# Router logits from the un-normalised rows, with the layer norm's root and mean entering per token behind the router

## The chip, the core and the metric

The kernel runs on one core of a Trainium2 chip. The metric is the time of one execution on the device in microseconds (us), taken as the median of several runs; lower is better. The core has five engines with instruction streams of their own: TensorE (PE) for matmuls and transposes, VectorE (DVE) and ScalarE (ACT) for elementwise work, GpSimd (POOL) as another elementwise engine, and SyncE (SP), which here issues the DMA transfers that bring the weights.

## The reference, cut to what matters

```python
def grouped_moe(x, router_w, router_bias, w_gate, w_up, w_down):
    x2 = x.reshape(-1, d)
    aff = jax.nn.sigmoid((x2 @ router_w).astype(jnp.float32))
    sel = (aff + router_bias.astype(jnp.float32)).reshape(-1, N_GROUPS, EXPERTS_PER_GROUP)
    grp_score = jnp.sum(lax.top_k(sel, 2)[0], -1)
    ...
    def step(acc, ew):
        g_e, wg_e, wu_e, wd_e = ew
        h = jax.nn.silu(x2 @ wg_e) * (x2 @ wu_e)
        return acc + (h @ wd_e) * g_e[:, None].astype(x2.dtype), None
...
    for l in range(DEPTH):
        ...
        x = layer_norm(ALPHA * x + mix, ln_mix_g[l], ln_mix_b[l])
        ffn = grouped_moe(x, router_w, router_bias, moe_w_gate[l], moe_w_up[l], moe_w_down[l])
        x = layer_norm(ALPHA * x + ffn, ln_ffn_g[l], ln_ffn_b[l])
    return x
```

There are 256 tokens of width 1024 and two layers. `mix` is a conformer convolution in layer 0 and a differential attention in layer 1. After each, a layer norm with gain and bias feeds a mixture of experts: a router of 16 columns picks two experts of one group for each token, and every expert is three matrices. A second block (a state space mixer with attention, then a feed-forward layer) follows; the change does not touch it.

## The kernel before, in words

The tokens lie as two blocks of 128 rows (`tb` 0 and 1), each row of 1024 columns handled as two halves of 512 (`nh` 0 and 1). All weights come from memory in units of 1 MB. SP issues them in the order of a fixed plan into ring buffers, as far ahead as the rings have room; a ring slot becomes free when the unit in it was used.

**Phase A** (layer 0's mixer): eight `pw1` units, for each of which ACT makes a rounded high part `wh` and POOL or DVE the remainder `wl` (L376), then PE multiplies (L381 to L383). Some columns of the depthwise convolution run on PE (`cv`, L623) with band matrices `band` that POOL writes (L599); their shifted inputs `xq` come back from memory by DMA. Then a layer norm, the projection `pw2`, and at its end the residual sum `res`.

**The head of each MoE** is what the change is about. The last unit of the last projection (`pw2` in layer 0, `wo` in layer 1) is computed as four groups of six matmuls, one for each block and half; behind each, DVE adds the group into the sum (L689 or L1218) and takes statistics (L429, L430). Behind the last group come 16 or 18 matmuls on zeros (`warm`, L359), which only keep PE at work, the variance's root (ACT's Ln and Exp L416 and L417, DVE L418 to L420), and the scaling of the rows in four halves, two on DVE (L440), two on ACT (L441). PE transposes the normalised rows (`fm_x1T`, L452), DVE (L742) and ACT (L744) put gain and bias on the way out of PSUM, and the router's matmuls (`lg`, L749) follow. Their sum is copied (`lgs`), added across four partition groups (`aff`, L754) and goes through a sigmoid. Beside it, rows are split for the experts: ACT writes the rounded `nh` (L735), DVE the remainder `nl` (L759).

**Routing** is a chain of small DVE instructions, from `sel` (L945) over ranks (`rkd_e`, `rk_e`, `rkd_g`, `rk_g`, L935 to L950) to the mask `maskb` (L956); PE makes positions of it (`pos`, L959), DVE a selection matrix `S` (L773), and PE's `px` (L787, L790) gathers the rows for the experts from `nh` and `nl`. The matrix units `u_moe` are used from the first `pg` (L812) on. No engine has other work to put under this chain.

Instructions stand on each engine in an order that is fixed when the program is built; each waits at its turn for what it needs.

Of the kernel before, what the change touches and what calls it, by code (L numbers as in the profile page):

```python
# [9 lines left out]
F32 = mybir.dt.float32  # L10
# [17 lines left out]
NE = 16  # L28
# [5 lines left out]
LN_EPS = 1e-5  # L34
# [37 lines left out]
COL_AT = {}  # L72
# [63 lines left out]
def pack(I):  # L136
    g = {k: np.asarray(v) for k, v in I.items()}
    a = {}
# [87 lines left out]
    a["wdown"] = units_q(g["w_down_2"][0])  # L226
    return {k: np.ascontiguousarray(v) for k, v in a.items()}


class Net:  # L230
# [229 lines left out]
    def build(self, phases="ABCDE"):  # L460
        tc, nc = self.tc, self.nc
        self.order(phases)
        with ExitStack() as ctx:
# [21 lines left out]
            c3 = ExitStack()  # L485
            xs = self.phase_a(late, early, c3) if "A" in phases else self.skip("n1", c3)
            for i in range(TB):
                self.dump(f"n1{i}", xs[i])
            rows = lambda l: self.rows.get(l) or self.mix_rows(l)
            if "B" in phases:  # L490
                xs, src = self.moe(0, xs, "mix_g0", "mix_b0", ["ring4", "ring5", "ring3"], rows(0))
            else:
                xs, src = self.inject("y1")
# [4 lines left out]
            self.retire = {}  # L498
            xs = self.attention(xs, c3) if "C" in phases else self.skip("n3", c3)
            for i in range(TB):  # L500
                self.dump(f"n3{i}", xs[i])
            if "D" in phases:
                xs, src = self.moe(1, xs, "mix_g1", "mix_b1", ["ring4", "ring5", "ring3", "ring2"], rows(1))
            else:
                xs, src = self.inject("y3")
# [62 lines left out]
    def phase_a(self, late, early, c3):  # L568
# [64 lines left out]
        taps, tap = conv_taps(), None  # L633
        rel_bias = self.rel_bias(e1)
        res = [self.act.tile([P, D], F32, tag=f"xacc{tb}", name=f"res{tb}") for tb in range(TB)]
        n = [self.act.tile([P, D], F32, tag=f"x{tb}", name=f"n{tb}") for tb in range(TB)]
        for j in range(KT):
# [51 lines left out]
        self.proj_q("pw2", range(4), sh, sl, lo=nc.gpsimd, done= lambda tb, nh, pp: nc.vector.tensor_tensor(  # L689
            res[tb][:, nh * 512:(nh + 1) * 512], pp, res[tb][:, nh * 512:(nh + 1) * 512], ALU.add))  # L690
        self.rows[0] = self.mix_rows(0)
        self.warm(W["l0"])
        self.norm_rows(res, "l0", AF.Sigmoid)
        late.close()
        self.open_ring(c3, "ring4", RING4)
        return res

# [24 lines left out]

    def moe(self, l, n, gname, bname, last_rings, rows):
        nc = self.nc
        with ExitStack() as ctx:
# [6 lines left out]
            for tb in range(TB):  # L732
                xnh.append(self.act.tile([P, D], FR, tag=f"x{tb}", name=f"nh_{l}{tb}"))
                xnl.append(b1.tile([P, D], FR, tag=f"nl{tb}", name=f"nl_{l}{tb}"))
                nc.scalar.activation(xnh[tb], n[tb], AF.Copy)  # L735
            g_row, b_row = rows
            x1T = b1.tile([P, KT, T], F32, tag="xe", name=f"x1T{l}")

            def evac(j, pt):
                d = x1T[:, j]  # L740
                if j // 2 % 2 == 0:
                    nc.vector.tensor_scalar(d, pt, self.col(gname, j), self.col(bname, j), op0=ALU.mult, op1=ALU.add)  # L742
                else:
                    nc.scalar.activation(d, pt, AF.Identity, bias=self.col(bname, j), scale=self.col(gname, j))  # L744
            self.to_fm(n, evac, f"x1T{l}")
            lg = self.bank(f"lg{l}")
            for k in range(KT):
                r = slice(32 * (k % 4), 32 * (k % 4) + 32)
                nc.tensor.matmul(lg[r, :T], self.col("router_w", NE * k, 32), x1T[:, k], start=k < 4, stop=k >= 4)  # L749
            lgs = b1.tile([P, T], F32, tag="h", name=f"lgs{l}")  # L750
            nc.scalar.activation(lgs, lg[:, :T], AF.Copy)
            pa = self.bank(f"aff{l}")
            for tb in range(TB):
                nc.tensor.matmul(pa[:, tb * NE:(tb + 1) * NE], lgs[:, tb * P:(tb + 1) * P], self.col("groups", 0, NE), start=True, stop=True)  # L754
            aff = b1.tile([P, TB, NE], F32, name=f"affs{l}")
            nc.scalar.activation(aff, pa[:, :TB * NE].rearrange("p (t e) -> p t e", t=TB), AF.Sigmoid)
            self.warm(W["lg"])
            for tb in range(TB):
# [3 lines left out]
            nc.gpsimd.tensor_copy(idg[:, :, :P], self.ident.unsqueeze(1).to_broadcast([P, TB, P]))  # L762
            posm, nmax, gates = self.route(l, b1, aff)
# [266 lines left out]
    def attention(self, n, c3):  # L1030
# [165 lines left out]
        for tb in range(TB):  # L1196
# [659 lines left out]
```

## Time and profile before

| | |
|---|---|
| median of 3 runs | 1167.34 us (1165.78 to 1167.7) |
| the profiled execution | 1166.63 us |
| its span, first to last instruction | 1164.9 us |
| granted TensorE clock, mean | 0.990 of full speed |
| PE busy | 1112.4 us, 95% |
| DVE, ACT, POOL busy | 631.8, 455.3, 308.1 us (54%, 39%, 26%) |
| DMA | 315.11 MB, 271 GB/s over the span |

The span is what the trace's rows sum to; 1.7 us of the execution lie outside it. PE's 95% is an average over stages with different limits: beside the weights' DMA, the span has stretches in which PE and DMA wait together for a chain of small steps.

### The profile page before, as it was taken

Reading aid. Unit: us, or ns where it says so; the run is one execution under the profiler, and the core shown is the slowest. Engines: PE = TensorE matmul, PEld = TensorE weight load, DVE = VectorE, ACT = ScalarE, POOL = GpSimd, SP = SyncE. Lnnn points to the kernel's source line nnn. Section 1 sums busy time; section 2 is a strip of 40 time slices with the busy share of each in tenths; the row PEclk is TensorE's granted clock in tenths of the full one; section 3 lists DMA queues with packets and bytes.
Section 4 is the critical chain, followed back from the end, with each engine's and each line's share of the span. In section 5 each row is a group of like instructions: output and inputs, shape, how many; then the busy total and the mean of one; then the engine's idle time right before and its main releaser. Section 6 shows DMA issues by size and latency. Waiting matters only on the chain.

```text
span 1164.9 us, 18257 instructions
## 1 busy us (share of the span) xinstructions
PE 1112.4 (95%) x7235; PEld 790.8 (68%) x7235; DVE 631.8 (54%) x1259; ACT 455.3 (39%) x798; POOL 308.1 (26%) x187
## 2 busy tenths in 40 slices
PE   9879989999999998989999999999999999999996
PEld 7857434444337997434344337989999988999996
DVE  6936721232227766721233227866988858665555
ACT  4314311011216665311011116555677566444443
POOL 5922000000003432000000005552324574444443
PEclk9989999999999999999999999999999999999998
DMA  9989489999999645599999993443323452554551
GB/s 358 308 260 403 152 364 418 420 419 421 419 415 415 238 161 218 240 372 387 419 419 421 419 418 106 161 155 118 128 92 109 173 208 73 217 181 167 196 199 55
DMA packets 53215, 315.11 MB, mean 271 GB/s; under 512 B 7111, under 2 KB 13312, under 8 KB 17024
## 3 DMA queue, kind: packets, MB, share of 16 engines
q1 hardware_dynamic: 49016, 309.02, 68.3%
q10 hardware_dynamic: 4104, 4.82, 1.3%
q8 instruction: 60, 0.98, 0.3%
q14 instruction: 35, 0.29, 0.1%
HBM read 312.01 MB, written 3.39 MB: 271 GB/s over the span
## 4 chain that ended last, share of the span: by engine, by line
PE 41%; DVE 9%; ACT 3%; DMA 1%; issue 1%; POOL 0%; ACTq 0%; DVEq 0%; POOLq 0%; SPq 0%
PE up L382 4%; PE up L383 4%; PE py L812 4%; PE up L381 4%; PE pu L812 4%; PE pg L812 3%; DVE E L1548 2%; PE pdn L383 2%; PE pdn L382 2%; PE pdn L381 2%; PE dwin L381 1%; PE dwin L382 1%; PE dwin L383 1%; DVE dwin L1342 1%; PE dwout L383 1%; PE dwout L382 1%
## 5 line engine op out<-in xcount | busy, mean ns | idle before, releaser
L812 PE MATMUL pu<-u_moe,xe 128*64 128x512 f32 x256 | 114.6, 600 | 4.7 <-PEq L991 4.7
L812 PE MATMUL py<-u_moe,hT 128*64 128x512 f32 x256 | 114.0, 596 | 1.4 <-DMA u_moe<-in_moe 0.8
L813 PE MATMUL pu<-u_moe,xe 128*64 128x512 f32 x256 | 114.7, 600 | 0.0
L813 PE MATMUL py<-u_moe,hT 128*64 128x512 f32 x256 | 113.6, 596 | 0.0
L812 PE MATMUL pg<-u_moe,xe 128*64 128x512 f32 x256 | 113.4, 593 | 0.0
L813 PE MATMUL pg<-u_moe,xe 128*64 128x512 f32 x256 | 113.0, 593 | 0.0
L881 DVE TENSOR_TENSOR h<-h,pu 128x512 f32<-128x512 f32 x16 | 11.0, 688 | 184.3 <-PE pu L813 171.6
L381 PE MATMUL dwin<-xih,wh 128*128 128x272 f32 (+1 forms) x352 | 104.8, 298 | 1.1 <-DVE xih L1288 1.1
L382 PE MATMUL dwin<-xil,wh 128*128 128x272 f32 (+1 forms) x352 | 102.1, 290 | 1.1 <-DVE xil L1289 1.1
L382 PE MATMUL up<-fxl,wh 128*128 128x258 f32 (+1 forms) x352 | 100.5, 285 | 1.6 <-DVE fxl L1729 1.6
L383 PE MATMUL dwin<-xih,wl 128*128 128x272 f32 (+1 forms) x352 | 101.5, 288 | 0.0
L381 PE MATMUL up<-fxh,wh 128*128 128x258 f32 (+1 forms) x352 | 100.4, 285 | 0.8 <-ACT fxh L1728 0.8
L383 PE MATMUL up<-fxh,wl 128*128 128x258 f32 (+1 forms) x352 | 100.4, 285 | 0.0
L376 POOL TENSOR_TENSOR wl<-u_win,wh 128x1024 fp32r<-128x1024 f32 x25 | 60.3, 2412 | 62.6 <-ACT wh L367 59.9
L916 DVE SCALAR_TENSOR_TENSOR yl<-py,gc,yh 128x512 fp32r<-128x512 f32 x32 | 24.0, 751 | 94.7 <-ACT yh L915 93.7
L812 PEld LDWEIGHTS pu<-u_moe,xe 128*64 128x64 f32 x256 | 35.1, 138 | 59.2 <-issue 58.0
L812 PEld LDWEIGHTS py<-u_moe,hT 128*64 128x64 f32 x256 | 33.4, 137 | 59.9 <-issue 56.0
L812 PEld LDWEIGHTS pg<-u_moe,xe 128*64 128x64 f32 x256 | 34.6, 137 | 54.7 <-issue 53.6
L376 POOL TENSOR_TENSOR wl<-u_wup,wh 128x1024 fp32r<-128x1024 f32 x22 | 52.8, 2401 | 64.7 <-ACT wh L367 64.7
L382 PEld LDWEIGHTS up<-fxl,wh 128*128 128x128 f32 x352 | 67.7, 192 | 2.5 <-DVE fxl L1729 1.8
L381 PEld LDWEIGHTS up<-fxh,wh 128*128 128x128 f32 x352 | 67.6, 192 | 2.0 <-ACT fxh L1728 1.3
L382 PEld LDWEIGHTS dwin<-xil,wh 128*128 128x128 f32 x352 | 67.0, 190 | 2.0 <-DVE xil L1289 1.9
(526 smaller groups left out, 3025.6 us busy)
## 6 DMA issues: line engine op xcount, KB each, us to landing
u_moe<-in_moe SPq DMA_DIRECT2D x192, 1024.0 KB, 18.6
u_win<-in_win SPq DMA_DIRECT2D x22, 1024.0 KB, 4.9
u_wup<-in_wup SPq DMA_DIRECT2D x22, 1024.0 KB, 5.3
u_pw<-in_pw SPq DMA_DIRECT2D x11, 1024.0 KB, 11.6
u_wdown<-in_wdown SPq DMA_DIRECT2D x11, 1024.0 KB, 4.9
u_wout<-in_wout SPq DMA_DIRECT2D x8, 1024.0 KB, 4.9
u_wk<-in_wk SPq DMA_DIRECT2D x4, 1024.0 KB, 15.8
u_wq<-in_wq SPq DMA_DIRECT2D x4, 1024.0 KB, 16.2
```

The lines of the kernel that those rows point to most:

```text
L376: eng.tensor_tensor(l, w, h.bitcast(F32), ALU.subtract)
L381: mm(ps, lh, rh, start=first, stop=False)
L382: mm(ps, lh, rl, start=False, stop=False)
L383: mm(ps, ll, rh, start=False, stop=last)
L812: nc.tensor.matmul(ps[0:64], a, ra, start=first, stop=last)
L813: self.upped = nc.tensor.matmul(ps[64:128], b, rb, start=first, stop=last)
L881: nc.vector.tensor_tensor(h, h, pu, ALU.mult)
L916: nc.vector.scalar_tensor_tensor(yl[:, s], py[nh], gc, yh[:, s].bitcast(F32), op0=ALU.mult, op1=ALU.subtract)
L1342: nc.vector.scalar_tensor_tensor(pb, raw[:, k:k + L], wc(k), pb, op0=ALU.mult, op1=ALU.add)
L1548: nc.vector.tensor_scalar(E[:, q:q + w], a[:, i, q:q + w], nA[:, c, h:h + 1], 0.0, op0=ALU.add, op1=ALU.min)
```

## The change

A class `Head` takes over the end of the last projection and the head of the MoE. As each group of six matmuls is done, PE transposes the raw half row of the group before (`rt`, L242 of the changed kernel), ACT copies it out (`xr`, L243), and the router multiplies these raw columns by router weights that already hold the gain (`gw`, written once in phase A by POOL). The root r and the mean enter behind the router: sigmoid(r * sum - r * mean * c + d), with two rows c and d of 16 numbers (`cd`) that are prepared in phase A by a method `router` (eight small matmuls, a POOL spread, a `ones` matrix, one more matmul). The 16 transposes of normalised rows with their eight evacuations fall away, and so do the 16 and 18 `warm` matmuls; 3 come in the new head, and `lg` grows from 9 to 13. The rows are normalised whole, block 0 on DVE and block 1 on POOL (L296). `nl` goes from DVE to POOL in four halves (L304), and POOL's cast `idg` is put behind them. The core of the diff:

```diff
-W = dict(start=16, a=16, l0=16, lg=9, pos=(4, 6), f0=22, f1=22, l1=18, mix=20)
+W = dict(start=16, a=16, head=(1, 2), lg=13, pos=(4, 6), f0=22, f1=22, mix=20)
...
+    def turn(self, tb, nh):
+        bank = self.net.bank(f"rt{self.l}{tb}{nh}")
+        s = slice(nh * 512, nh * 512 + 512)
+        for j in range(4):
+            self.nc.tensor.transpose(bank[:, j * P:(j + 1) * P], self.res[tb][:, (4 * nh + j) * P:(4 * nh + j + 1) * P], self.net.ident)
+        self.nc.scalar.activation(self.xr[tb][:, s], bank, AF.Copy)
+
+    def done(self, tb, nh, pp):
+        nc = self.nc
+        x = self.res[tb][:, nh * 512:nh * 512 + 512]
+        nc.vector.tensor_tensor(x, pp, x, ALU.add)
+        nc.vector.bn_stats(self.st[tb][:, nh], x)
+        if nh:
+            nc.vector.bn_aggr(self.mv[:, tb], self.st[tb])
+        if self.due:
+            self.turn(*self.due)
+        self.due = (tb, nh)
...
+    def last(self):
+        net, nc, l = self.net, self.nc, self.l
+        self.lg = net.bank(f"lg{l}")
+        self.logits(0, range(KT))
+        net.warm(W["head"][0])
+        self.turn(*self.due)
+        v = net.tiny.tile([P, TB], F32, tag="bnv", name=f"v_l{l}")
+        nc.vector.tensor_scalar(v, self.mv[:, :, 1], LN_EPS, None, op0=ALU.add)
+        self.r = net.rsqrt_act(v, [P, TB], f"l{l}")
+        self.nmr = net.tiny.tile([P, TB], F32, tag="nmr", name=f"nmr_l{l}")
+        nc.vector.scalar_tensor_tensor(self.nmr, self.mv[:, :, 0], -1.0, self.r, op0=ALU.mult, op1=ALU.mult)
+        self.logits(1, range(4))
+        net.warm(W["head"][1])
+        self.logits(1, range(4, KT))
+
+    def gates(self, b1):
...
+        for tb in range(TB):
+            nc.vector.scalar_tensor_tensor(lin[:, tb], net.cd[:, l, 0], self.nmr[:, tb:tb + 1], net.cd[:, l, 1], op0=ALU.mult, op1=ALU.add)
+        for tb in range(TB):
+            self.lin = nc.vector.scalar_tensor_tensor(lin[:, tb], pa[:, tb * NE:(tb + 1) * NE], self.r[:, tb:tb + 1], lin[:, tb], op0=ALU.mult, op1=ALU.add)
+        aff = b1.tile([P, TB, NE], F32, name=f"affs{l}")
+        nc.scalar.activation(aff, lin, AF.Sigmoid)
+        return aff
+
+    def rows(self, xnh, xnl):
+        nc = self.nc
+        for tb in range(TB):
+            i = (nc.gpsimd if tb else nc.vector).tensor_scalar(self.res[tb], self.res[tb], self.mv[:, tb, 0:1], self.r[:, tb:tb + 1], op0=ALU.subtract, op1=ALU.mult)
+            if not tb:
+                self.net.after(i, self.lin)
+            self.net.tc.keep_in_program_order(nc.scalar.activation(xnh[tb], self.res[tb], AF.Copy))
+        low = None
+        for h in range(2):
+            s = slice(512 * h, 512 * h + 512)
+            for tb in range(TB):
+                i = nc.gpsimd.tensor_tensor(xnl[tb][:, s], self.res[tb][:, s], xnh[tb][:, s].bitcast(F32), ALU.subtract)
+                low = self.net.after(i, low) if low else i
+        self.low = low
...
+    def router(self, pool, pin):
...
+        self.after(nc.gpsimd.memset(ones, 1.0), pin())
+        nc.gpsimd.tensor_tensor(spread, self.col("groups", 0, NE).unsqueeze(1).to_broadcast([P, 4, NE]), part.unsqueeze(2).to_broadcast([P, 4, NE]), ALU.mult)
+        pd = self.bank("cds")
+        nc.tensor.matmul(pd[:, :4 * NE], ones, spread.rearrange("p c e -> p (c e)"), start=True, stop=True)
...
-            for tb in range(TB):
-                self.tc.keep_in_program_order(nc.vector.tensor_tensor(xnl[tb], n[tb], xnh[tb].bitcast(F32), ALU.subtract))
```

On POOL, at the head of layer 0's MoE (`wl` belongs to the last projection, the load is that of the branch on the largest count), before:

```order
L376 TENSOR_TENSOR wl<-u_pw_2_152,wh 128x1024 [waits DMAHW7_49,DVE_49,Activation_49]
L376 TENSOR_TENSOR wl<-u_pw_3_410,wh 128x1024 [waits DMAHW1_49,Activation_49]
L762 CAST idg_1408<-cst_m 128x2x128 [waits DVE_49,PE_49]
L990 TENSOR_LOAD nmax_1439 [waits DVE_49]
L991 COMPARE_AND_BRANCH
```

and after:

```order
L455 TENSOR_TENSOR wl<-u_pw_3_414,wh 128x1024 [waits DMAHW1_49,Activation_49]
L296 TENSOR_SCALAR res_176<-res_176,mv_l_1165,y_l_1351 128x1024 [waits DVE_49,PE_49]
L304 TENSOR_TENSOR nl_1394<-res_175,nh_1393 128x512 [waits Activation_49,Pool_49]
L304 TENSOR_TENSOR nl_1396<-res_176,nh_1395 128x512 [waits Activation_49]
L304 TENSOR_TENSOR nl_1394<-res_175,nh_1393 128x512
L304 TENSOR_TENSOR nl_1396<-res_176,nh_1395 128x512
L842 CAST idg_1432<-cst_m 128x2x128
```

Five large instructions stand where one small cast stood, behind the norm's root and behind ACT's copies.

On DVE, the same place in the changed kernel, from the norm's last small step to the start of routing:

```order
L271 SCALAR_TENSOR_TENSOR nmr_l_1358<-mv_l_1165,y_l_1351 128x2 [waits DVE_49]
L286 SCALAR_TENSOR_TENSOR lin_1403<-cd,nmr_l_1358 128x16 [waits DVE_49]
L286 SCALAR_TENSOR_TENSOR lin_1403<-cd,nmr_l_1358 128x16
L288 SCALAR_TENSOR_TENSOR lin_1403<-aff_1400,y_l_1351,lin_1403 128x16 [waits DVE_49,PE_49]
L288 SCALAR_TENSOR_TENSOR lin_1403<-aff_1400,y_l_1351,lin_1403 128x16 [waits DVE_49]
L296 TENSOR_SCALAR res_175<-res_175,mv_l_1165,y_l_1351 128x1024
L1025 TENSOR_TENSOR sel_1434<-affs_1408,row_router_b 128x32 [waits Activation_49]
```

Where two half norms, four evacuations and two `nl` of 128x1024 stood ahead of `sel`, there are now four instructions of 128x16 and one norm of 128x1024.

On PE in phase A, at the change from `pw_5` to the next convolution, in the changed kernel:

```order
L461 MATMUL pw_5_584<-xl,wh 128x256
L462 MATMUL pw_5_584<-xh,wl 128x256
L654 MATMUL cds<-ones_m 128x64 [waits DVE_49,Pool_49]
L722 MATMUL cv_678<-xq_403,band_401 32x256 [waits DMAHW4_49,DMAHW3_49,DMAHW5_49,DMAHW2_49,DVE_49]
L722 MATMUL cv_678<-xq_403,band_401 32x256 x31
L460 MATMUL pw_6_714<-xh,wh 128x256 [waits DVE_49,Activation_49]
```

and on POOL the `ones` matrix that `cds` waits for:

```order
L455 TENSOR_TENSOR wl<-u_pw_6_144,wh 128x1024 [waits PE_49,Activation_49]
L455 TENSOR_TENSOR wl<-u_pw_7_146,wh 128x1024 [waits DMAHW4_49,PE_49,Activation_49]
L651 MEMSET ones_m 128x128
L698 TENSOR_TENSOR band_662<-cst_m,cols_a 128x1024 [waits PE_49]
```

Before, `cv` followed `pw_5` directly; now a matmul stands between them whose operand POOL writes only behind the first `wl` of `pw1`'s last unit.

## Rows read from the trace of the kernel before

**Rows 1.** Windows: length, busy us of PE, PEld, DVE, ACT, POOL, clock, DMA share, GB/s.

```profile
125.00:130.00 5.00, 3.40 (x23) 1.30 (x20) 3.06 (x5) 3.56 (x9) 0.00 (x0) 1.00 0.13 52
...
200.00:385.00 185.00, 182.06 (x931) 89.35 (x926) 68.11 (x140) 43.86 (x80) 15.78 (x8) 1.00 1.00 413
```

**Rows 2.** Waits of SP's queue, 120 to 145 us: total, times, longest.

```profile
SPq L317 <- PE pg L813: 9.9, 3, 7.3
```

**Rows 3.** Timeline, head of layer 0's MoE: start, us, what, [idle before <- releaser].

```profile
118.58 0.39 PE L383 MATMUL pw<-wh,sl 128*128 128x512 f32 x1
...
121.96 0.16 DVE L437 SCALAR_TENSOR_TENSOR nmr_l<-mv_l,y_l 128x2 f32<-128x2 f32 x1
122.04 1.00 DVE L440 TENSOR_SCALAR res<-res,mv_l,y_l 128x512 f32<-128x512 f32 x2
...
122.73 2.16 PE L452 MATMUL fm_x1T<-cst_m,res 128*128 128x128 f32 x16 [0.26 <-DVE res L440]
...
124.08 1.99 ACT L735 ACTIVATE nh<-res 128x1024 fp32r<-128x1024 f32 x2
...
125.62 2.35 DVE L759 TENSOR_TENSOR nl<-res,nh 128x1024 fp32r<-128x1024 f32 x2
...
129.50 2.12 PE L359 MATMUL warm<-warm_b 128*128 128x512 bf16 x9
...
129.91 0.19 DVE L945 TENSOR_TENSOR sel<-affs,row_router_b 128x32 f32<-128x32 f32 x1 [1.94 <-ACT affs L756]
...
132.30 0.19 DVE L956 SCALAR_TENSOR_TENSOR maskb<-rk_g,top 128x32 bf16<-128x32 f32 x1
...
132.55 0.18 PE L959 MATMUL pos<-maskb,cst_mb 128*128 128x16 bf16 x1 [0.93 <-DVE maskb L956]
...
133.80 0.36 PE L787 MATMUL px<-S,nh 128*128 128x256 f32 x1
```

**Rows 4.** POOL's groups by shape, the whole span: count, busy us, mean ns.

```profile
L1818 POOL TENSOR_TENSOR o<-o,hm 128x512 f32<-128x512 f32 x3 | 3.7, 1260 | 9.0 <-DVE o L1817 9.0
...
L1739 POOL COPY sqa_f<-sq_f 128x258 f32<-128x258 f32 x1 | 0.4, 401 | 4.9 <-ACT sq_f L1735 4.9
```

**Rows 5.** Timeline of attention, DVE and POOL side by side, three places.

```profile
395.17 2.40 POOL L376 TENSOR_TENSOR wl<-u_wq,wh 128x1024 fp32r<-128x1024 f32 x1 [3.24 <-ACT wh L367]
...
396.19 0.41 DVE L1131 TENSOR_REDUCE m<-e 128x1 f32<-128x256 f32 x1
...
420.00 2.92 POOL L376 TENSOR_TENSOR wl<-u_wk,wh 128x1024 fp32r<-128x1024 f32 x1 [7.36 <-ACT wh L367]
...
420.55 2.39 DVE L419 SCALAR_TENSOR_TENSOR t_sub<-t_sub,ss 128x4 f32<-128x4 f32 x1
...
446.44 0.16 DVE L419 SCALAR_TENSOR_TENSOR t_sub<-t_sub,ss 128x4 f32<-128x4 f32 x1
446.49 2.41 POOL L376 TENSOR_TENSOR wl<-u_wo,wh 128x1024 fp32r<-128x1024 f32 x1 [6.97 <-ACT wh L367]
...
446.64 2.29 DVE L420 SCALAR_TENSOR_TENSOR y_sub<-t_sub,y_sub 128x4 f32<-128x4 f32 x1
```

**Rows 6.** Timeline of phase A, POOL and PE, 44 to 65 us.

```profile
44.61 4.80 POOL L376 TENSOR_TENSOR wl<-u_pw,wh 128x1024 fp32r<-128x1024 f32 x2
...
44.94 3.66 PE L623 MATMUL cv<-xq,band 128*32 128x256 f32 x64
...
59.33 5.35 PE L623 MATMUL cv<-xq,band 128*32 128x256 f32 x64 [4.78 <-DMA xq<-hd]
```

**Rows 7.** Windows: the stretch behind PE's idle time in phase A.

```profile
60.00:65.00 5.00, 5.00 (x63) 3.12 (x55) 4.65 (x11) 0.27 (x1) 0.22 (x1) 0.69 0.51 172
```

**Rows 8.** Timeline, end of attention's last projection (layer 1), DVE and PE.

```profile
464.75 0.62 PE L383 MATMUL wo<-wh,col 128*128 128x512 f32 x2
...
465.19 0.69 DVE L1218 TENSOR_TENSOR y<-wo,y 128x512 f32<-128x512 f32 x1 [1.44 <-PE wo L383]
```

**Rows 9.** Timeline, near the end of layer 0's MoE, PE.

```profile
343.31 0.64 PE L812 MATMUL py<-u_moe,hT 128*64 128x512 f32 x1 [0.83 <-DMA u_moe<-in_moe]
```

More of the change, by code (lines that the diff above doesn't have):

```diff
@@ L485, in build @@
             c3 = ExitStack()
-            xs = self.phase_a(late, early, c3) if "A" in phases else self.skip("n1", c3)
-            for i in range(TB):
-                self.dump(f"n1{i}", xs[i])
+            xs, head = self.phase_a(late, early, c3)
             rows = lambda l: self.rows.get(l) or self.mix_rows(l)
             if "B" in phases:
-                xs, src = self.moe(0, xs, "mix_g0", "mix_b0", ["ring4", "ring5", "ring3"], rows(0))
+                xs, src = self.moe(0, xs, head, "mix_g0", "mix_b0", ["ring4", "ring5", "ring3"], rows(0))
             else:
@@ L498, in build @@
             self.retire = {}
-            xs = self.attention(xs, c3) if "C" in phases else self.skip("n3", c3)
-            for i in range(TB):
-                self.dump(f"n3{i}", xs[i])
+            xs, head = self.attention(xs, c3)
             if "D" in phases:
-                xs, src = self.moe(1, xs, "mix_g1", "mix_b1", ["ring4", "ring5", "ring3", "ring2"], rows(1))
+                xs, src = self.moe(1, xs, head, "mix_g1", "mix_b1", ["ring4", "ring5", "ring3", "ring2"], rows(1))
             else:
@@ L660, in phase_a @@
                 next(rel_bias, None)
+            if j in (2, 3, 5):
+                next(router, None)
             if j in (5, 6):
@@ L688, in phase_a @@
         self.preload("natural_log_exp_and_others")
-        self.proj_q("pw2", range(4), sh, sl, lo=nc.gpsimd, done= lambda tb, nh, pp: nc.vector.tensor_tensor(
-            res[tb][:, nh * 512:(nh + 1) * 512], pp, res[tb][:, nh * 512:(nh + 1) * 512], ALU.add))
+        head = Head(self, 0, res)
+        self.proj_q("pw2", range(4), sh, sl, lo=nc.gpsimd, done=head.done)
         self.rows[0] = self.mix_rows(0)
-        self.warm(W["l0"])
-        self.norm_rows(res, "l0", AF.Sigmoid)
+        head.last()
         late.close()
         self.open_ring(c3, "ring4", RING4)
-        return res
+        return res, head
     def proj_q(self, nm, units, ah, al, done, pp=None, lo=None):
@@ L734, in moe @@
                 xnl.append(b1.tile([P, D], FR, tag=f"nl{tb}", name=f"nl_{l}{tb}"))
-                nc.scalar.activation(xnh[tb], n[tb], AF.Copy)
             g_row, b_row = rows
[L737 to L752, printed above, removed]
-            for tb in range(TB):
-                nc.tensor.matmul(pa[:, tb * NE:(tb + 1) * NE], lgs[:, tb * P:(tb + 1) * P], self.col("groups", 0, NE), start=True, stop=True)
-            aff = b1.tile([P, TB, NE], F32, name=f"affs{l}")
-            nc.scalar.activation(aff, pa[:, :TB * NE].rearrange("p (t e) -> p t e", t=TB), AF.Sigmoid)
+            aff = head.gates(b1)
+            head.rows(xnh, xnl)
             self.warm(W["lg"])
-            for tb in range(TB):
-                self.tc.keep_in_program_order(nc.vector.tensor_tensor(xnl[tb], n[tb], xnh[tb].bitcast(F32), ALU.subtract))
             idg = b1.tile([P, TB, P + 2 * NE], FR, name=f"idg{l}")
             identr = idg[:, 0, :P]
-            nc.gpsimd.tensor_copy(idg[:, :, :P], self.ident.unsqueeze(1).to_broadcast([P, TB, P]))
+            self.after(nc.gpsimd.tensor_copy(idg[:, :, :P], self.ident.unsqueeze(1).to_broadcast([P, TB, P])), head.low)
             posm, nmax, gates = self.route(l, b1, aff)
@@ L1230, in attention @@
         self.rows[1] = self.mix_rows(1, False)
-        self.warm(W["l1"])
-        self.norm_rows(xacc, "l1", AF.Sigmoid)
+        head.last()
         late.close()
         self.open_ring(c3, "ring4", RING4)
-        return xacc
+        return xacc, head
     def second(self, n):
```

49 lines of the change are left out of this document (44 added, 5 removed).

## The prediction

> **What bounds the kernel now.** I read the page's table of slices first, then the windows, then the waits and the timeline of the stretch that changes. In the long body of the first MoE both weights and PE are full: of 185 us PE is busy 182 and the DMA engines all of it [rows 1]. At its head nothing is full: from 125 to 130 us PE works 3.40 of 5 us, DVE 3.06, ACT 3.56, and the DMA share is 0.13, because the rings are full and SP waits up to 7.3 us for a `pg` to free a slot [rows 1, 2]. So the transfers start again only when the first expert consumes a unit, and the transfers then set the pace: what the head gains or loses is carried to the end of the stage nearly whole. The head is a chain: last matmul of `pw2` at 118.58, norm, transposes, logits, `sel` at 129.91, `maskb` at 132.30, `px` at 133.80 [rows 3]. From the last group to `px` it takes 15.2 us, twice in the kernel, and that is what the change can win from. Phase A, the third place touched, is PE bound up to a wait for shifted inputs.
>
> **The change, part by part: the chain up to `sel`.** Removed: 16 transposes (2.16 us) that waited for the normalised rows, eight evacuations behind them, and the `nl` on DVE (2.35) [rows 3]. Put in instead, ahead of the norm's root: two groups of four transposes between the projection's groups, at a quarter of 2.16 each about 0.5, so the projection ends 0.9 to 1.1 later. The third and fourth group lie behind it. ACT's last copy of a half row, half of an `nh` copy of 1.0 by [rows 3], stands ahead of Ln and Exp on ACT and delays the root by about 0.5. `nmr`, 121.96 before [rows 3], comes at about 123.4. The logits and their sum run beside these steps and are ready by then.
>
> Now the order rows count. POOL's norm of block 1 is released by the same root, and so runs against DVE's `lin`. The trace has no such one-input instruction of 1024 columns on POOL; 401 ns for 258 columns [rows 4] scale to 1.6 us; 2.40 for two inputs of 1024 [rows 5] is the upper bound, and 0.4, the row unscaled, the lower. I take 1.5, by the scaled row, since some of the 401 ns will not grow. DVE's norm of block 0 is two of the former halves, 1.00 [rows 3], and stands ahead of `sel`. 123.4 plus 1.5 plus small steps and 1.00 puts `sel` at about 126.2, against 129.91: **3.7 earlier**. ACT's `nh` copies (1.99 for two, so 1.0 each [rows 3]) start when a block is normalised, ending at 127.3 and 128.3.
>
> **Routing beside `nl` on POOL.** From `sel` to `maskb` are 2.39 us of short DVE steps [rows 3]. Four `nl` of 128x512 now become ready from 127.3 on, inside this chain; one takes 1.26 [rows 4]. What happens to a short DVE instruction beside a long one on POOL is in [rows 5]: at 420.55 a step of 128x4, 0.16 at 446.44, lasts 2.39 and ends where POOL's `wl`, begun at 420.00, ends. At 446.49 POOL slips in between two dependent DVE steps, and the second, 446.64, lasts 2.29, again to POOL's end. A reduction at 396.19, under a `wl` of 2.40 from 395.17, runs on in 0.41. So for steps with two inputs the engines exclude each other.
>
> The Trainium skill, GPSIMD Engine Reference, section 1 (Specifications), says that POOL's SBUF interfaces are shared with VectorE and contended by DVE instructions that have two SBUF inputs or run in a two-port mode. The trace agrees: it is the 128x4 step with two inputs that stretches, 0.16 to 2.39, and the reduction with one that does not.
>
> Without exclusion `maskb` would come at 126.2 + 2.4 = 128.6. With it each of the four `nl` gets in at one of the gaps between dependent steps: 4 x 1.26 = 5.0, of which some 0.6 (three reductions of about 0.2) lies over steps that run on: 4.4. That gives 133.0 against 132.30: **0.7 later** instead of 3.7 earlier. The cast `idg` behind them can take another 0.4 from the steps to `px`; I leave it as part of the bound. The price per layer lies between 0 (POOL never finds a gap) and 5.4.
>
> **PE's clock.** The 13 `warm` matmuls last 13/9 of 2.12 [rows 3], 3.1 us, from the end of `aff` near 123.9 to 127.0; then PE idles to `pos` near 133.2, 6 us where it was 0.93 before [rows 3]. The nearest row: PE idles 4.78 us before 59.33 and the 64 matmuls behind last 5.35, where the same number took 3.66 at 44.94 [rows 6], at a granted clock of 0.69 over 5 us [rows 7], a mixture of the levels 1.2 and 2.4 GHz. That is 1.7 us; I take 1.2, since `px` is only 32 and pays for its evacuations too, with bounds 0 and 1.7. Of the 3.7 us earlier case nothing of this would remain, since `pos` would come at 128.8, 1.8 idle.
>
> **Layer 1.** The same head, with one more wait: PE works groups 00 and 01 there in turns and ends both at once, the last two matmuls of both from 464.75 on, and DVE's add of group 00 runs from 465.19 for 0.69 [rows 8]. The transposes of half 00 stand right behind group 01 and wait for that add: PE stalls about 0.7, and the groups behind it move with it. So layer 0: 0.7 + 1.2 = **+1.9**; layer 1: 0.7 + 0.7 + 1.2 = **+2.6**.
>
> **Phase A.** POOL gets three multiplications and two fills; at 0.40 us for 258 columns and 1.26 for two inputs of 512 [rows 4] they come to about 1.1 us, and POOL stands in two `wl` of 2.40 from 44.61 to 49.41 [rows 6], so I let all of it delay them. PE's `cds` waits for the `ones` fill, which stands behind the first half of `pw1_7`, so it can run at about 50.6 (49.41 and 1.1), where the convolution began at 44.94: PE stalls 5.7 us. The cover is PE's wait of 4.78 before 59.33 [rows 6], for a DMA that does not depend on this stall; what is left is 0.9, and the next convolution, behind a shorter idle time, loses or gains with the clock up to 1.7. I take **+1.0**, bounds 0 and 5.7 (no cover at all). The gain's multiplication itself costs nothing: POOL does it under PE's `pw1` matmuls; without that cover it is 1 us.
>
> **DMA near the end of the MoE.** One PE wait on a unit of 0.83 [rows 9] shows PE and DMA nearly tied; a later head gives transfers no head start but a branch moved later in SP's queue does. I take **-0.5**, bounds -0.8 and 0.
>
> **Sum** against the profiled execution of 1166.63: +1.9 + 2.6 + 1.0 - 0.5 = +5.0, so 1171.6. The median of the runs is 0.7 above that execution, less than their spread; I leave it.
>
> **The rivals.** *POOL loses the race (faster).* If DVE's chain keeps POOL out (the `wl` at 420.00 had itself to wait for DVE, 2.92 instead of 2.40 [rows 5], so neither engine has a fixed right), or `nl` is ready after `maskb`, then layer 0 is 3.7 earlier and layer 1 3.0, with phase A's +1.0 and tie -0.3: -6.0, 1160.6. The chain decides by 3.7 per layer; the sign turns once more than about three of the four `nl` fall within it. Against it: the copies end at 127.3 and 128.3, before the chain would end at 128.6, and one gap is enough for each [rows 5].
>
> *Blocked, but PE keeps its clock and phase A is fully covered (no change).* Then 0.7 + 1.4 + 0.3 - 0.5 = +1.9: 1168.5. For it: `warm` matmuls run up to 6 us ahead of `px`, and four more stand behind `pos`; against it, the gap of 4.78 and the clock behind it [rows 6, 7].
>
> *Worse.* POOL's norm takes 2.40 instead of 1.5, 0.9 in each layer, and phase A loses 3 instead of 1: 1171.6 + 1.8 + 2.0 = 1175.4.
>
> **How the numbers follow.** Blocked as summed 0.38, worse 0.09, blocked with the clock kept 0.21, not blocked 0.32. A measurement here can tell about 0.2% (2.3 us) from no change, so slower 0.47, same 0.21, faster 0.32. The time is that of the likeliest case, 1171.6, which by itself spans 1169 to 1174; as the faster case holds more than 2 in 10, the range reaches down to it, and up to the worse one: 1160 to 1176.
>
> **What would show it.** In the profile of the changed kernel: the `nl` rows on POOL at 1.26 each with one routing step of DVE stretched to the same end (right), or all routing steps at their old length (wrong); `sel` near 126 in layer 0; `maskb` within 1 us of 132.3 from the projection's old end; an idle time of PE before `pos` of 5 to 6 us and a granted clock well under 1 behind it; `cds` waiting for POOL over 5 us, with PE's wait before the convolution at 59 gone; transposes in layer 1 waiting for DVE's add. If the routing chain keeps 2.4 us, the prediction is wrong by about 11 us, to the faster side.

## The result: slower by 1.0%

| | before | after |
|---|---|---|
| median | 1166.56 us (1163.36 to 1167.7, 4 runs) | 1176.9 us (1176.54 to 1183.7, 4 runs) |
| the profiled execution | 1166.63 us | 1183.7 us |
| its span | 1164.9 us | 1181.9 us |
| granted clock, mean | 0.990 | 0.977 |

The ratio is 1.0102 with a 95% interval of 1.0064 to 1.014. The medians differ by 10.3 us, where +5.0 was predicted, and 1176.9 lies 0.9 us above the range. The execution that was profiled is the longest of the four, 6.8 us over the median. So mechanisms are read from it, and sums over stretches from a second profile of the same kernel in the experiments (1179.58 us).

The changed kernel's page, busy time of each engine over the span:

```profile
PE 1112.4 (94%) x7258; PEld 795.5 (67%) x7265; DVE 634.3 (54%) x1253; ACT 454.1 (38%) x796; POOL 326.1 (28%) x202
```

PE is busy for 1112.4 us, to the tenth what it was, though the `warm` matmuls take 4.8 us less in all (33.4 against 38.2); the rest takes that much more, in part at a lower clock (0.977 against 0.990). So the loss is to be sought in the times in which PE waits, and in the clock behind them.

**The head of layer 0's MoE.** Timeline of the changed kernel (start, us, engine, line, what, [idle before <- releaser]), to hold against [rows 3]:

```profile
124.97 0.40 PE L462 MATMUL pw<-wh,sl 128*128 128x512 f32 x1
...
128.88 3.78 POOL L296 TENSOR_SCALAR res<-res,mv_l,y_l 128x1024 f32<-128x1024 f32 x1 [11.78 <-DVE nmr_l L271]
...
128.92 1.17 DVE L286 SCALAR_TENSOR_TENSOR lin<-cd,nmr_l 128x16 f32<-128x16 f32 x2
...
131.02 0.18 DVE L1025 TENSOR_TENSOR sel<-affs,row_router_b 128x32 f32<-128x32 f32 x1
...
131.23 0.29 DVE L1015 TENSOR_TENSOR rkd_e<-sel 128x128 f32<-128x128 f32 x1
...
132.63 4.93 POOL L304 TENSOR_TENSOR nl<-res,nh 128x512 fp32r<-128x512 f32 x4
...
132.75 1.20 DVE L1015 TENSOR_TENSOR rkd_g<-gs 128x32 f32<-128x32 f32 x1
...
133.98 1.18 DVE L1016 TENSOR_TENSOR rkd_g<-rkd_g,cst_m 128x32 f32<-128x32 f32 x1
135.20 0.18 DVE L1018 TENSOR_REDUCE rk_g<-rkd_g 128x8 f32<-128x32 f32 x1
135.42 0.97 DVE L1036 SCALAR_TENSOR_TENSOR maskb<-rk_g,top 128x32 bf16<-128x32 f32 x1
136.31 1.30 DVE L1036 SCALAR_TENSOR_TENSOR mask<-rk_g,top 128x32 f32<-128x32 f32 x1
136.44 0.17 PE L1039 MATMUL pos<-maskb,cst_mb 128*128 128x16 bf16 x1 [4.09 <-DVE maskb L1036]
...
138.79 0.55 PE L867 MATMUL px<-S,nh 128*128 128x256 f32 x1 [0.96 <-DVE gsum L1056]
```

From the start of the projection's last matmul to `sel` it takes 6.05 us where it was 11.33. But while POOL makes its four `nl`, four steps of DVE with two inputs, about 0.19 each before, take 1.20, 1.18, 0.97 and 1.30; the reduction between them keeps its 0.18. PE idles 4.09 us before `pos`, then the clock falls. Windows from `px` to the first `pg`, of the changed kernel (columns as in [rows 1]):

```profile
138.80:144.60 5.80, 5.80 (x28) 5.69 (x28) 2.26 (x7) 1.23 (x3) 0.00 (x0) 0.55 0.01 3
```

and of the kernel before:

```profile
133.80:137.80 4.00, 4.00 (x29) 3.56 (x29) 2.18 (x7) 1.28 (x3) 0.00 (x0) 1.00 0.01 2
```

The same 32 matmuls (a few records are missing) take 5.80 us at a granted clock of 0.55 and 4.00 at 1.00.

**Phase A.** Timeline of the changed kernel:

```profile
50.24 0.69 PE L654 MATMUL cds<-ones_m 128*128 128x64 f32 x2 [4.81 <-POOL ones_m L651]
...
64.05 0.48 DVE L750 SCALAR_TENSOR_TENSOR hp<-pw,cols_a,sg 128x256 f32<-128x256 f32 x1 [6.89 <-ACT sg L749]
64.45 9.41 DVE L713 SCALAR_TENSOR_TENSOR conv<-hp,cols_a,conv 128x256 f32<-128x256 f32 x18
...
73.60 2.37 POOL L455 TENSOR_TENSOR wl<-u_pw,wh 128x1024 fp32r<-128x1024 f32 x1 [5.36 <-ACT wh L446]
73.77 3.29 DVE L455 TENSOR_TENSOR wl<-u_pw,wh 128x1024 fp32r<-128x1024 f32 x1
...
76.98 0.47 DVE L750 SCALAR_TENSOR_TENSOR hp<-pw,cols_a,sg 128x256 f32<-128x256 f32 x1
...
88.58 5.74 PE L722 MATMUL cv<-xq,band 128*32 128x256 f32 x64 [9.37 <-DMA xq<-hd]
```

and the same four places of the kernel before:

```profile
57.07 0.48 DVE L650 SCALAR_TENSOR_TENSOR hp<-pw,cols_a,sg 128x256 f32<-128x256 f32 x1
...
68.81 1.23 DVE L376 TENSOR_TENSOR wl<-u_pw,wh 128x1024 fp32r<-128x1024 f32 x1 [1.94 <-ACT wh L367]
...
72.03 0.48 DVE L650 SCALAR_TENSOR_TENSOR hp<-pw,cols_a,sg 128x256 f32<-128x256 f32 x1 [2.00 <-ACT sg L649]
...
83.56 5.33 PE L623 MATMUL cv<-xq,band 128*32 128x256 f32 x64 [4.55 <-DMA xq<-hd]
```

PE's stall of 4.81 us, with the low clock behind it, makes the gate `hp` (DVE's product of a unit's output with its sigmoid `sg`) behind `pw_6` 7.0 us later (57.07 to 64.05): the convolution behind the stall takes 5.83 us at a granted clock of 0.62, where it took 3.66 at 1.00. Behind that gate on DVE stand 18 taps of the convolution, 9.41 us, then a `wl`, then the gate behind `pw_7`, whose result goes to memory and comes back as the last `xq`. The `wl` takes 3.29 us instead of 1.23, because DVE now reaches it while POOL makes a `wl` of its own (73.60 to 75.97): the same hold-up as in the head. ACT has the last gate's input `sg` ready at 73.89, and DVE comes to that gate at 76.98. So 2.1 of the 4.95 us by which this gate is late are POOL's `wl`. In every run with `cds` behind `pw_5` DVE's `wl` takes 3.28 or 3.29 us, and 1.23 in every run with `cds` behind `pw_7`. The last convolution `cv`, which needs that `xq`, now begins 5.0 us later, and PE waits 9.37 us before it.

**The branch.** While the first experts are at work, the program tests the largest number of tokens that one expert got and, if it is over the capacity, runs a slow path. Each engine has this branch in its instruction stream. On SP it stood behind the unit `u_moe_29`; in the changed kernel it stands behind `u_moe_33`, and the load of the count, which stood behind `u_moe_18`, with it. This is in SP's order before and after:

```
66 L317 DMA u_moe_29_1603<-in_moe 128x2048
67 L991 COMPARE_AND_BRANCH
```

```
68 L396 DMA u_moe_33_1658<-in_moe 128x2048
69 L1070 TENSOR_LOAD nmax_1463
70 L1071 COMPARE_AND_BRANCH
```

Waits of the changed kernel, 140 to 200 us (what waited <- for what: us in total, times, longest):

```profile
DVE S L853 <- SPq L1071: 11.5, 1, 11.5
...
PE px L867 <- DVE S L853: 4.4, 1, 4.4
```

DVE's next selection `S` waits 11.5 us for SP's branch, and PE waits 4.4 us for `S`. `S` shares its ring of buffers with the chunks that the slow path loads (both have the tag `S`), which ties it to the branch although the path isn't taken. In the kernel before, DVE's wait at this place is 0.9 us, and it is for PE's branch.

**Where the 12.9 us of the two spans went** (start of the named instruction on PE's timeline, kernel before against the second profile of the changed one, 1164.9 and 1177.8 us):

| stretch | before | after | difference |
|---|---|---|---|
| start to the end of phase A's convolution (`ty`) | 88.83 | 94.22 | +5.4 |
| `ty` to first `px`, layer 0 | 44.97 | 44.54 | -0.4 |
| `px` to `pg` | 3.97 | 5.65 | +1.7 |
| `pg` to second `px` (the branch) | 42.92 | 46.39 | +3.5 |
| to layer 1's attention (`fm_x2T`) | 171.62 | 170.59 | -1.0 |
| to the last matmul of `wo` | 116.09 | 116.86 | +0.8 |
| to first `px`, layer 1 | 15.54 | 13.81 | -1.7 |
| `px` to `pg` | 3.96 | 5.18 | +1.2 |
| `pg` to second `px` (the branch) | 44.68 | 47.26 | +2.6 |
| to the second block (`fm_hT`) | 171.44 | 173.48 | +2.0 |
| to the end | 460.88 | 459.82 | -1.1 |

The profile of the result (1181.9 us) is 4.1 us longer than this second one. Of these, 3.1 lie in the stretches to `fm_x2T` and to the last matmul of `wo`, in none of the places named so far.

The two stretches of the branch hold a second thing beside PE's wait for `S`. At its own branch PE idles some 2.3 us in both kernels, and behind that the granted clock falls in one layer and not in the other. Windows of the kernel before, layer 0, of the changed kernel (second profile), layer 0, and of the kernel before, layer 1:

```profile
137.70:180.70 43.00, 39.94 (x183) 14.78 (x181) 12.06 (x21) 4.03 (x7) 0.00 (x0) 1.00 0.82 329
...
144.40:190.80 46.40, 41.66 (x181) 15.32 (x180) 11.78 (x21) 3.96 (x7) 0.00 (x0) 0.96 0.84 341
...
487.90:532.60 44.70, 41.59 (x182) 15.32 (x181) 12.06 (x21) 3.96 (x7) 0.00 (x0) 0.96 0.81 317
```

The same matmuls keep PE busy for 39.94 us at a clock of 1.00 and for 41.6 at 0.96. In layer 0 it is the changed kernel that has the lower clock, in layer 1 the kernel before (the changed one is busy for 39.98 there). So of the +3.5 in layer 0, 1.7 are PE's wait for `S` and 1.7 this clock; of layer 1, where PE waits 4.0 us for `S`, the clock takes 1.6 off. By PE's waits the branch is 1.7 + 4.0 = 5.7 us.

### The profile page after: what moved, and what is told of

Same layout as the page of the kernel before. It is cut to its first block, busy times and chain, and to the rows that moved or that the text cites. A ratio compares the mean times of both kernels' runs of the same rounds, so it can differ in the third digit from the quotient of the medians.

```text
span 1181.9 us, 18324 instructions
## 1 busy us (share of the span) xinstructions
PE 1112.4 (94%) x7258; PEld 795.5 (67%) x7265; DVE 634.3 (54%) x1253; ACT 454.1 (38%) x796; POOL 326.1 (28%) x202
## 4 chain that ended last, share of the span: by engine, by line
PE 39%; DVE 7%; ACT 3%; issue 1%; POOL 1%; DMA 1%; ACTq 0%; DVEq 0%; POOLq 0%
PE up L461 4%; PE py L892 4%; PE up L462 4%; PE up L460 4%; PE pg L892 3%; PE pu L892 3%; PE pdn L462 2%; PE pdn L461 2%; PE pdn L460 2%; DVE E L1627 2%; PE dwin L461 1%; PE dwin L462 1%; PE dwin L460 1%; PE dwout L462 1%; PE dwout L461 1%
## 5 line engine op out<-in xcount | busy, mean ns | idle before, releaser
L892 PE MATMUL pu<-u_moe,xe 128*64 128x512 f32 x256 | 112.9, 593 | 3.8 <-PEq L1071 2.2
L893 PE MATMUL pu<-u_moe,xe 128*64 128x512 f32 x256 | 113.0, 593 | 0.0
L462 PEld LDWEIGHTS dwin<-xih,wl 128*128 128x128 f32 x352 | 66.9, 190 | 1.8 <-POOL wl L455 1.8
```

The lines of the kernel that those rows point to most:

```text
L462: mm(ps, ll, rh, start=False, stop=last)
L892: nc.tensor.matmul(ps[0:64], a, ra, start=first, stop=last)
L893: self.upped = nc.tensor.matmul(ps[64:128], b, rb, start=first, stop=last)
```

## The experiments

The first four ran on one chip, as did the next three and the last three, each set with its own runs of the kernel before: 1167.8, 1167.49 and 1166.26 us. The ratios are those on record with each result; they differ from the quotients of the medians by up to 0.2%.

**The same kernel again (e1_again).** No edit.

> The changed kernel itself once more, since its profiled execution (1183.7 us) lies 6.8 above the other three. Theory (three places): the last convolution of phase A ends near 94.3 us again (88.9 before), the second px of the first MoE starts near 191 us (180.7 before), and px behind the head runs at a low clock; what the profiled run had on top of 1176.9 is in one of these three or behind the second MoE. Rival (all in the heads, by exclusion of POOL and DVE): the two heads carry 4 to 5 us each and phase A and the branch little. Time 1176 to 1178 by both.

Measured: 1180.89 us, ratio 1.0126 (1.0101 to 1.0152). The slowdown is there again, 13.1 us between the medians; the time itself lies above the 1176 to 1178 expected. Waits of DVE, 170 to 200 us:

```profile
DVE S L853 <- SPq L1071: 11.2, 1, 11.2
```

PE's waits for `S` are 1.7 us in layer 0 and 4.0 in layer 1.

**The `ones` matmul placed later (e2_cds_late).** The third part of the router's preparation stands behind `pw_7` instead of `pw_5`.

```diff
-            if j in (2, 3, 5):
+            if j in (2, 3, 7):
                 next(router, None)
```

> The matmul cds and its ones fill moved from behind pw1_5 to behind pw1_7, all else as in the changed kernel. Theory: the stall ahead of pw1_6 made DVE's convolution taps 7 us late and with them the last input for PE's convolution; without it phase A ends as before, near 89 us, and the time falls by 4 to 6 us, to 1171 to 1173. Rival (PE's wait for xq covers the stall, the loss lies in the heads): 1176 to 1177.

Measured: 1172.11 us, ratio 1.0045 (1.0024 to 1.0067), 8.8 us less than e1. PE's timeline:

```profile
74.13 0.69 PE L654 MATMUL cds<-ones_m 128*128 128x64 f32 x2 [3.65 <-DMA hd<-hp]
74.75 11.80 PE L722 MATMUL cv<-xq,band 128*32 128x256 f32 x192
```

The place of this one matmul carries all of phase A's loss. Phase A's convolution ends at 86.49, 7.7 us earlier than in e1 and 2.3 us earlier than even before the change: the last three convolutions run back to back, where PE waited 1.15 and 4.55 us between them (the second is in the rows of before above). PE spends 3.65 us of that in front of `cds`. The last `xq` is in time here because it was issued at 74.27 against 75.44: the store `hd` ahead of it landed after 1.80 us, where it took 2.83. Why the store was faster is open.

**The branch back in its place (e3_branch_early).** The lag with which SP's loads are written into the program is raised by four around the branch.

```diff
+                if p == 1:
+                    self.LAG += 4
                 pg = up(p, 0, xe, "pg")
...
                     self.overflow(l, b1, xnh, xnl, identr, gname, bname, posm, gates, nmax, xacc)
+                    self.LAG -= 4
```

> SP's branch on the largest count stands four units earlier in SP's queue (behind u_moe_29, where it stood before the change, instead of u_moe_33); all else as in the changed kernel. Theory: DVE's next S waits for the end of SP's branch, which drains all transfers in flight; four units fewer make it end 8 to 10 us earlier, PE's wait of 4.4 us before the second px goes in both layers, and the time falls by 6 to 9 us, to 1168 to 1171. Rival (the transfers set the pace of the MoE, so the wait is given back): 1175 to 1177.

Measured: 1172.34 us, ratio 1.0044 (1.0026 to 1.0062), 8.5 us less than e1. SP's branch stands behind `u_moe_29` again. Waits of DVE, 170 to 200 us:

```profile
DVE S L853 <- SPq L1074: 1.5, 1, 1.5
```

11.2 became 1.5, and PE waits for `S` no more. From `pg` to the second `px` it gains 1.8 us in layer 0 and 4.4 in layer 1, close to the 1.7 and 4.0 that PE had waited for `S`. The two profiled executions differ by 4.7 us (1174.91 and 1179.58), the medians by 8.5; the branch's price lies between these, with the 6.2 of the two stretches in the middle. SP's waits at its branch line, 140 to 200 us, e1:

```profile
SPq L1071 <- SPq L1071: 14.4, 2, 11.9
```

and e3:

```profile
SPq L1074 <- SPq L1074: 11.8, 4, 5.1
```

At its branch SP waits in one stretch of 11.9 us where it was at most 5.1. The trace's records of SP name what for: eight semaphores one after the other, and they are the eight on which the kernel's transfers report that they have landed. The last wait that takes time ends with the last unit issued ahead of the branch. In e1 that unit is issued at 174.29 and lands at 189.64, and SP goes on at 189.66; in e3 it is issued at 167.25 and lands at 180.16, and SP goes on at 180.17; in the kernel before it lands at 172.89, and SP goes on at 172.91. So in these profiles SP stays at the branch until all that it issued ahead of it has landed, and four more units ahead of it move that moment from 42.0 us behind the first `px` (e3) to 50.9 (e1).

**`nl` back on DVE, but behind the routing chain (e4_nl_dve).** In four halves of 128x512, ordered behind `S`; the cast `idg` on POOL is no longer tied to them.

```diff
-                i = nc.gpsimd.tensor_tensor(xnl[tb][:, s], self.res[tb][:, s], xnh[tb][:, s].bitcast(F32), ALU.subtract)
-                low = self.net.after(i, low) if low else i
+                prev = self.net.after(nc.vector.tensor_tensor(xnl[tb][:, s], self.res[tb][:, s], xnh[tb][:, s].bitcast(F32), ALU.subtract), prev)
...
             st = select(0)
+            head.lows(self.picked)
```

> nl taken from POOL and put on DVE behind the selection matrix S, in four halves. In the built program SP's load of the count stands behind u_moe_18 again, as before the change. Theory: maskb comes within 2.4 us of sel (it took 5.4 in the changed kernel), px starts 1 to 2 us earlier in each head, the clock falls less, and SP's branch is early again: 2 + 2 + 7 us less, 1165 to 1169. Rival (exclusion by POOL is harmless): no gain beyond the branch's, 1170 or so; if the branch is harmless too, 1176.

Measured: 1165.57 us, ratio 0.9985 (0.9965 to 1.0004), 15.3 us less than e1. Timeline of its head:

```profile
129.69 0.18 DVE L1030 TENSOR_TENSOR sel<-affs,row_router_b 128x32 f32<-128x32 f32 x1
...
131.42 0.19 DVE L1020 TENSOR_TENSOR rkd_g<-gs 128x32 f32<-128x32 f32 x1
...
132.09 0.19 DVE L1041 SCALAR_TENSOR_TENSOR maskb<-rk_g,top 128x32 bf16<-128x32 f32 x1
132.34 0.17 PE L1044 MATMUL pos<-maskb,cst_mb 128*128 128x16 bf16 x1 [1.32 <-DVE maskb L1041]
```

All routing steps have their old 0.19, and PE's idle time before `pos` is 1.32. But this edit is not one thing: in the built program SP's branch stands behind `u_moe_29` as well, so the 15.3 us hold the branch's price too. Phase A's convolution still ends late (92.92).

**Both (e5_both).** The edits of e2 and e4.

> The changed kernel with both repairs: cds and its fill behind pw1_7, and nl on DVE behind S. Theory (the costs add: 7 to 9 us from phase A, 15 from nl with the branch): 1157 to 1160, faster than before by 8 to 10 us; phase A ends near 86.6, px starts about 6 us earlier than before. Rival (the repairs overlap, the transfers set the pace): 1163 to 1166.

Measured: 1155.66 us (1152.96 to 1157.67), ratio 0.9893 (0.9871 to 0.9915): faster than either kernel. From `ty` to `px` it takes 40.66 us, 4.3 less than before the change, and in layer 1 from `wo`'s last matmul to `px` 10.00 us, 5.5 less. From 128.2 to 132.4, from `px` to `pg`, the windows show a clock of 1.00:

```profile
128.20:132.40 4.20, 3.65 (x21) 2.75 (x21) 4.20 (x11) 0.17 (x1) 0.00 (x0) 1.00 0.01 4
```

**The preparation alone (e6_before_router).** The kernel before with the method `router` called at the same three places; its results are not used.

```diff
+        router = self.router(e1, lambda: glu)
...
+            if j in (2, 3, 5):
+                next(router, None)
```

> The kernel before with only the preparation of the router's rows in phase A added (gain products, eight small matmuls, spread, ones fill, cds, at the places of the changed kernel); its results are unused. Theory: cds waits for POOL 4.8 us, pw1_6 and DVE's taps come 7 us later, phase A ends 5.4 us later and the time rises by 4 to 6 us, to 1171 to 1174. Rival (PE's wait for xq covers it): 1166 to 1168, as before.

Measured: 1170.58 us, ratio 1.0035 (1.0013 to 1.0057). PE's timeline:

```profile
50.20 0.69 PE L582 MATMUL cds<-ones_m 128*128 128x64 f32 x2 [4.82 <-POOL ones_m L579]
...
87.77 5.74 PE L650 MATMUL cv<-xq,band 128*32 128x256 f32 x64 [8.97 <-DMA xq<-hd]
```

The same two waits in a kernel in which nothing else changed; phase A's convolution ends at 93.44, 4.6 us later than before. The medians differ by 3.1 us.

**More matmuls on zeros (e7_warm30).** 30 instead of 13 behind the logits, to keep PE at work up to `pos`.

```diff
-W = dict(start=16, a=16, head=(1, 2), lg=13, pos=(4, 6), f0=22, f1=22, mix=20)
+W = dict(start=16, a=16, head=(1, 2), lg=30, pos=(4, 6), f0=22, f1=22, mix=20)
```

> The changed kernel with 30 instead of 13 matmuls on zeros between aff and pos, so that PE does not idle there; in its built program SP's load of the count stands behind u_moe_18, as before the change, so it is to be compared with the run of the early branch (1172.3), not with the changed kernel. Theory: pos at the same distance from the projection's end, px at full clock, 1.5 us less in each layer, 1168.5 to 1170. Rival (the clock behind the idle time costs nothing, or is given back by the transfers): 1171.5 to 1173.

Measured: 1172.33 us, ratio 1.0042 (1.002 to 1.0064). The 8.6 us below e1 are no verdict on the clock: in the built program SP's branch is behind `u_moe_29` here too, and against e3, which differs from e1 in just that (1172.34), nothing is gained. DVE's and PE's timeline shows why not:

```profile
138.32 0.31 DVE L1052 TENSOR_TENSOR gates<-affs,mask 128x32 f32<-128x32 f32 x1
...
139.72 0.18 DVE L1049 SCALAR_TENSOR_TENSOR posm<-pos,mask 128x32 f32<-128x32 f32 x1
...
140.51 0.36 PE L867 MATMUL px<-S,nh 128*128 128x256 f32 x1 [2.23 <-DVE S L853]
```

The idle time before `pos` is 0.40. But on DVE the steps on `gates` stand ahead of `posm` now, which starts 2.6 us behind `pos` where it was 1.5 in the changed kernel, and PE idles 2.23 us before `px`. Behind that the granted clock from 142 to 148 us is 0.74. From `px` to `pg` it takes 4.7 and 4.6 us in the two layers, 1.4 and 0.6 less than in e3, and the stretches ahead of `px` are 1.1 us longer each. So the clock's term was not isolated; the test is inconclusive.

**The branch still earlier (e8_branch_earlier).** The lag of e3 on top of e5.

> Both repairs (the run at 1155.7 us) with SP's branch four units earlier still, behind u_moe_25. Theory (no px waits for the branch any more, so its place matters only while S waits): within 1.5 us of 1155.7. Rival (the drain's gap in the transfers itself costs time): 2 to 5 us less.

Measured: 1156.67 us, ratio 0.9899 (0.9846 to 0.9953). The condition of the expectation was not met: in the built order the branch stands behind `u_moe_29`, as in e5, so the run is e5 a second time and tells nothing new of the branch.

**Block 1's norm on DVE too (e9_norm_dve).** On top of e5.

```diff
-            i = (nc.gpsimd if tb else nc.vector).tensor_scalar(self.res[tb], self.res[tb], self.mv[:, tb, 0:1], self.r[:, tb:tb + 1], op0=ALU.subtract, op1=ALU.mult)
-            if not tb:
-                self.net.after(i, self.lin)
+            self.lin = self.net.after(nc.vector.tensor_scalar(self.res[tb], self.res[tb], self.mv[:, tb, 0:1], self.r[:, tb:tb + 1], op0=ALU.subtract, op1=ALU.mult), self.lin)
```

> Both repairs with the norm of block 1 on DVE behind that of block 0 instead of on POOL. POOL's norm lasts 3.78 us and the second lin beside it 1.01 instead of 0.2. Theory (lin is held by POOL's norm): lin back near 0.2, sel within 0.1 us of its old distance, since DVE's 0.8 for the norm takes the place of the 0.8 that lin waited; time within 1.5 us of 1155.7. Rival (lin waits for something else): lin stays at 1.0 and sel comes 0.8 later, 1 to 3 us more.

Measured: 1157.29 us, ratio 0.9904 (0.9871 to 0.9937), the same as e5 and e8. DVE's timeline:

```profile
121.14 0.38 DVE L286 SCALAR_TENSOR_TENSOR lin<-cd,nmr_l 128x16 f32<-128x16 f32 x2
...
122.06 1.53 DVE L296 TENSOR_SCALAR res<-res,mv_l,y_l 128x1024 f32<-128x1024 f32 x2
```

The first two `lin` take 0.38 together, where they take 1.17 beside POOL's norm. That gain and the second norm's 0.77 on DVE cancel.

**The two placements without `nl` (e10_cds_branch).** The edits of e2 and e3; `nl` stays on POOL in the chain.

> The changed kernel with cds behind pw1_7 and SP's branch behind u_moe_29, nl left on POOL inside the routing chain. Theory (three costs that add): 1180.9 - 8.8 - 8.5 = 1163.6, still 7 to 8 us above the version with nl on DVE, and DVE's rkd_g steps at 1.2 us. Rival (nl on POOL costs only by the branch): 1155 to 1158.

Measured: 1165.1 us, ratio 0.9992 (0.9966 to 1.0017). The two gains nearly add up: from the ratios of e1, e2 and e3 0.9963 would follow. Against e2, from which it differs in the branch alone, the ratio is 0.5% lower. Its head still shows the exclusion:

```profile
124.07 4.93 POOL L304 TENSOR_TENSOR nl<-res,nh 128x512 fp32r<-128x512 f32 x4
...
124.20 1.20 DVE L1018 TENSOR_TENSOR rkd_g<-gs 128x32 f32<-128x32 f32 x1
...
127.88 0.17 PE L1042 MATMUL pos<-maskb,cst_mb 128*128 128x16 bf16 x1 [4.10 <-DVE maskb L1039]
```

Against e5, e8 and e9, 1155.66 to 1157.29, it is some 8 to 9 us longer. That is the price of `nl` on POOL, with the cast `idg` behind it and with its clock, both layers together.

## Why the prediction was wrong, point by point

**Right: POOL holds up the routing chain.** The prediction took one routing step of DVE to be held for each `nl`, 4.4 us in all. Four steps are held, one for each, and from `sel` to `px` it takes 7.77 us where it was 3.89, so 3.9. `sel` was to be 3.7 earlier. It is 5.3 earlier counted from the projection's last matmul, 4.3 without the 1.0 by which two groups of transposes lengthen the projection. So layer 0's head comes out at -0.4 instead of +0.7, and layer 1's at -0.9 (-1.7 and +0.8) instead of +1.4. The 0.8, in the stretch that ends with `wo`, is no clear effect: in e6, where nothing of this stretch was changed, it is 1.1 us longer than in the kernel before. The rival in which POOL loses the race fell with that, and what it would have given is seen in e5: 4.3 and 5.5 us.

**Right: the clock.** 1.2 us in each layer was taken, and `px` to `pg` is longer by 1.7 and 1.2, behind 4.09 us of idle time where 5 to 6 had been expected. As e7 was inconclusive, that the idle time causes this rests on the two granted clocks, 0.55 and 1.00, and on the runs side by side: with 0.9 to 1.5 us of idle time before `pos` (the kernel before, e4, e5, e8, e9) `px` to `pg` takes 3.96 to 4.13 us, and with 4.1 (the changed kernel, e1, e2, e3, e10) 4.84 to 6.05.

**Right in kind, not in size: the wait for DVE's add in layer 1.** In the changed kernel the first transposes come directly behind that add:

```profile
477.64 0.69 DVE L248 TENSOR_TENSOR y<-wo,y 128x512 f32<-128x512 f32 x1 [1.42 <-PE wo L462]
...
478.39 0.66 PE L242 MATMUL rt<-cst_m,y 128*128 128x128 f32 x4
```

But PE has no idle time of note before them, since the last matmuls of group 01 (three, the last from 478.12) run beside the add. Of the predicted 0.7 next to nothing was paid.

**The first step that failed: phase A's cover.** The prediction saw PE's stall before `cds` (5.7 expected, 4.81 measured) and set against it "PE's wait of 4.78 before 59.33", "for a DMA that does not depend on this stall". That wait did disappear. But PE was not the only engine whose work the stall delayed. The stall also delayed the gate behind `pw_6` on DVE, and through DVE's 9.41 us of taps, and a `wl` that POOL now held up, the last gate, its store and the last `xq`. There PE's wait grew from 4.55 to 9.37. The loss was not covered but handed on, and came out three convolutions later: +5.4 instead of +1.0. The prediction's upper bound of 5.7 held; e2 and e6 settle the cause.

**The second step that failed: the sign of the branch's term.** "A branch moved later in SP's queue does" was to give transfers a head start, -0.5. It did the opposite. PE waits 1.7 and 4.0 us for it in the two layers, and e3 takes 4.7 (profiles) to 8.5 us (medians) off. The order of SP's queue had been read for what SP issues, and not for what SP itself waits for at its branch, the landing of all that it has issued, and for who waits until SP is past it, DVE's `S`. Why the program's builder moved the branch at all is open. The edits of e4 and e7, which don't name it, moved it back.

**The sum.** With the measured terms, -0.4 + 1.7 in layer 0, -0.9 + 1.2 in layer 1, +5.4 in phase A and +3.5 + 2.6 at the branches come to +13.1, against 12.9 between the spans. (The branches' 6.1 are 5.7 of waiting and 0.4 that holds the two clocks of before.) The stretches not named here (-1.0, +2.0 and -1.1) nearly cancel; the 2.0 at the end of layer 1 isn't explained, but that stretch takes between 170.9 and 173.8 us over all profiles of this document. The range was too narrow above: its case "worse" let phase A lose 3 where its own bound was 5.7, and the branch had no bound on the side of a loss.

## What to carry to other kernels

When a stall is laid "under" a wait of the same engine, follow what the stalled engine hands to the others: the wait is only cover if everything that ends it starts independently of the stall. When the built order moves a branch or another synchronising instruction in a DMA queue, ask what it waits for, which transfers are issued ahead of it, and who shares a buffer with what is inside it. And elementwise work that is given to POOL to relieve DVE belongs where DVE has no chain of short steps with two inputs; moving `nl` behind `S` and `cds` behind `pw_7`, which also left SP's branch in its old place, turned +1.0% into -1.1%.

## What the runs showed of the hardware that was not expected

POOL's instruction with one tensor input, the norm of 128x1024, takes 3.78 us, more than its `wl` with two inputs of that size (2.37); 1.5 had been estimated from the 401 ns of a 258-column copy [rows 4], and 2.40 given as the upper bound [rows 5]. It hardly shows in the time of e5 against e9; in the changed kernel POOL's first `nl` begins when it ends (132.63), 0.4 us after ACT's `nh` of block 0 was ready. Under it DVE's `sel` and `rkd_e`, with two inputs, run at 0.18 and 0.29. Only the `lin` at its beginning are stretched (1.17 for two, 0.38 without it). So "POOL is busy" is not enough to stretch DVE's steps; under the `nl`, with two inputs, every DVE step with two inputs was held.
